# Stick-breaking attention: two value matmuls in place of three, with the columns added afterwards

## The chip, the cores and the metric

The kernel runs on one core of one Trainium2 chip. A core has a matmul engine (TensorE, PE in the profile, with its weight loads shown apart as PEld), three engines for elementwise work (VectorE: DVE, ScalarE: ACT, GpSimd: POOL), a queue for transfers (SP), and 16 DMA engines that carry them. The time is the device time of one run in microseconds (us). Matmul results land in PSUM, which is cut into banks of 512 fp32 columns; all other tiles lie in SBUF.

## The reference, cut to what matters

The program is one layer of a residual trunk with 2048 rows of 1024: a projection, four heads of differential attention, eight heads of stick-breaking attention, an output projection, and a gated feed-forward layer. The change touches stick-breaking attention alone:

```python
z = jnp.einsum('bqhd,bkhd->bhqk', qb, k).astype(jnp.float32) * scale      # 64 wide heads
log_1mb = jnp.where(mask, jax.nn.log_sigmoid(-z), 0.0)
rem = lax.cumsum(log_1mb, axis=3, reverse=True) - log_1mb
a = jnp.where(mask, jnp.exp(jax.nn.log_sigmoid(z) + rem), 0.0)            # probabilities
y = jnp.einsum('bhqk,bkhd->bqhd', a.astype(v.dtype), v)
y_sb = rms_norm(y, sb_out_norm_w)                                         # per head, over 64 columns
```

The mask is strictly causal, so row block i (128 rows, i from 0 to 15) needs i + 1 key blocks of 128.

## The kernel before, in words

Inputs are fp32, and matmuls run on pairs of fp16 numbers. A value a is held as a high part and a low part, and a product a times v is computed as high times high, high times low and low times high, all added in PSUM.

Work is done in eight groups. Groups 0 to 3 are the differential heads, and groups 4 to 7 hold two stick-breaking heads each (m = 0 and 1). While a group's attention runs, the projection of the next group (L320 on PE, with its results split on ACT and DVE, L327 and L330) runs between. In the last group the output projection takes that place (L761 on PE, L764 on DVE). The feed-forward layer follows from about 1500 us on.

A unit of stick-breaking attention is one row block i, one head m, and up to 1024 keys (b). `stage_a` makes its scores on PE in chunks of 512 keys (L448, with the mask added at L450). ACT takes two sigmoids of each chunk (L554 and L555), DVE a running product from the right (L557, the TENSOR_TENSOR_SCAN of the profile) and a product (L558). `split_t` makes the high part on ACT (L89) and the low part on POOL (L98) into a buffer s16 (three of them). A transposing DMA on SP's queue (L403) then brings both parts to the tile aT, in which keys lie on partitions: tiles j hold the high parts, and nb + j the low parts.

`stage_b` runs five units later. Its `pv` (L458) multiplies the 128x128 tiles of aT, as stationary operands, with the values, which lie side by side as 64 high and 64 low columns for each head. For each key block it has three matmuls of 64 columns, each with a weight load of its own, into the same 64 columns of the PSUM tile yp. One yp tile of 512 columns holds four row blocks with two heads each (two row blocks in group 7, where k is 2), and there are two such tiles in turn.

When the last row block of a yp tile is done, `finish` norms it: ACT squares it into an SBUF tile y (L418), DVE sums the squares (L419), ACT and POOL make the inverse root (L148, L151), DVE multiplies yp by it into y (L429), PE transposes y back into yp (L431), and ACT and DVE split the result (L435, L436), which goes out by DMA (L439).

The order of the instructions on each engine is fixed when the program is built. A scheduler places them by a modelled timeline, and every engine then works through its list in that order. A small planner (`note`, `pick`) adds up estimated nanoseconds for each engine and by them decides which of two engines takes some of the splits.

Of the kernel before, what the change touches and what calls it, by code (L numbers as in the profile page):

```python
# [59 lines left out]
def block(tc, a, out):  # L60
# [3 lines left out]
    with top:  # L64
# [8 lines left out]
        def note(e, ns):  # L73
            load[e] += ns * KW[e]
# [176 lines left out]
        with ExitStack() as ph1:  # L251
# [152 lines left out]
                return aT  # L404

            @pri("fin")
            def finish(g, G, i, k, yp, ssum=None):
                nh, w = (1, 128) if g < 4 else (2, 64)
                nr = k * nh
                yv = yp[:, : k * P].rearrange("p (r e) -> p r e", e=w)  # L410
                y = sp.tile([P, 512], F32, tag="y", bufs=2, name=nm("y"))
                y_ = y[:, : k * P].rearrange("p (r e) -> p r e", e=w)
                ss = sm.tile([P, 8], F32, tag="yss", name=nm("yss"))
                if nh == 1:
                    for r in range(nr):
                        ACT.activation(y_[:, r, :], yv[:, r, :], AF.Square, accum_out=ss[:, r : r + 1])
                else:
                    ACT.activation(y_, yv, AF.Square)  # L418
                    DVE.tensor_reduce(ss[:, :nr], y_, op=ALU.add, axis=AX.X)  # L419
                rs = sm.tile([P, 8], F32, tag="yrs", name=nm("yrs"))  # L420
                if ssum is None:
                    rstd(rs[:, :nr], ss[:, :nr], 1.0 / w, G["epsy"][:])
                else:
                    er = sm.tile([P, 4], F32, tag="er", name=nm("er"))
                    ACT.activation(er[:, :k], ssum[:, :k, 0], AF.Square, scale=G["rty"][:])
                    DVE.scalar_tensor_tensor(rs[:, :nr], ss[:, :nr], 1.0 / w, er[:, :k], op0=ALU.mult, op1=ALU.add)
                    POOL.tensor_scalar(rs[:, :nr], rs[:, :nr], 1e-37, 0.0, op0=ALU.max, op1=ALU.add)
                    POOL.tensor_tensor(rs[:, :nr], rs[:, :nr], mhalf[:, :nr], ALU.pow)
                DVE.tensor_tensor(y_, yv, rs[:, :nr].unsqueeze(2).to_broadcast([P, nr, w]), ALU.mult)  # L429
# [6 lines left out]
                DVE.scalar_tensor_tensor(mo[:, :k, 1, :], tr, gn, mo[:, :k, 0, :], op0=ALU.mult, op1=ALU.subtract)  # L436
# [15 lines left out]
            @pri("pv")  # L452
            def pv(G, yp, y0, aT, b, n, o, wd, start, stop):
                nb = n // P
                for j in range(nb):
                    v = G["v"][2 * b + j // 4][:, j % 4, :]
                    for q, (a_, v_) in enumerate(((j, o), (j, o + wd), (nb + j, o))):
                        PE.matmul(yp[:, y0 : y0 + wd], lhsT=aT[:, a_, :], rhs=v[:, v_ : v_ + wd], start=start and j == 0 and q == 0, stop=stop and j == nb - 1 and q == 2, skip_group_check=True)  # L458

            def diff_attn(g, G):  # L460
                @pri("at")
# [74 lines left out]
            def sb_attn(g, G):  # L536
                last = {}

                @pri("at")
                def stage_a(i, m, b):  # L540
                    L = (i + 1) * 128
                    n = min(1024, L - 1024 * b)
                    be, om = z4(), z4()
                    if b == i // 8:
                        DVE.memset(om[:, n : n + 1], 8192.0)
                    else:
                        DVE.tensor_copy(om[:, n : n + 1], last[m][:, 0:1])
                    last[m] = om
                    for c in range((n - 1) // 512, -1, -1):
                        lo, hi = 512 * c, min(512 * c + 512, n)  # L550
                        w = hi - lo
                        sc = ps.tile([P, 512], F32, tag="sc", bufs=4, name=nm("sc"))
                        score_chunk(G, sc, i, 2 * b + c, m, w // P, b == i // 8 and hi == n)
                        ACT.activation(om[:, lo:hi], sc[:, :w], AF.Sigmoid, scale=G["nkz"][:])  # L554
                        ACT.activation(sc[:, :w], sc[:, :w], AF.Sigmoid, scale=G["kz"][:])  # L555
                        ov = om[:, lo:hi][:, ::-1]
                        DVE.tensor_tensor_scan(ov, ov, sc[:, :w], om[:, hi : hi + 1], op0=ALU.mult, op1=ALU.bypass)  # L557
                        DVE.tensor_tensor(be[:, lo:hi], sc[:, :w], om[:, lo + 1 : hi + 1], ALU.mult)  # L558
# [4 lines left out]
                ypd = {}  # L563

                def stage_b(i, m, b, n, aT):
                    r, k = fq(g, i)
                    if i // k not in ypd:
                        ypd[i // k] = ps.tile([P, 512], F32, tag="yp", name=nm("yp"))
                    yp = ypd[i // k]
                    pv(G, yp, P * r + 64 * m, aT, b, n, 128 * m, 64, r == 0 and m == 0 and b == i // 8, r == k - 1 and m == 1 and b == 0)  # L570
                    if m == 1 and b == 0 and r == k - 1:
                        finish(g, G, i, k, yp)
                        G["fin"] = i + 1

                pend = []
# [12 lines left out]
                for u in pend:  # L588
                    stage_b(*u)
# [638 lines left out]
```

## Time and profile before

| what | value |
|---|---|
| time, median of 3 runs | 2782.47 us (2777.36 to 2783.66) |
| span of the profiled execution (the only time that its page gives) | 2785.0 us |
| PE busy | 2489.9 us (89%), 17084 matmuls |
| DVE busy | 2000.8 us (72%) |
| ACT busy | 1361.8 us (49%) |
| POOL busy | 1445.2 us (52%) |
| L458, matmuls of both kinds of attention | 4896 matmuls, 281.2 us |
| mean granted TensorE clock | 0.966 |

Busy time counts every moment in which an engine has an instruction under way. Matmuls are pipelined, so a single one shows some 200 ns while a row of them runs at a much closer pace. The span is an average over stages: from 0 to about 610 us the projection and the differential heads, to about 1200 us the stick-breaking heads with the projection, to about 1500 us the last group with the output projection, and then the feed-forward layer.

### The profile page before, as it was taken

What the parts mean: (1) busy time and instruction counts of PE and PEld (TensorE: products, weight loads), DVE (VectorE), ACT (ScalarE), POOL (GpSimd) and SP (SyncE); (2) the same over time, 40 slices, a digit from 0 to 9 for tenths busy, and PEclk for the clock granted to TensorE, in tenths of its full rate; (3) what the DMA queues carried; (4) which work ended last, traced back from release to release, by engine and by line L of the source; (5) the groups of instructions that cost most, each with busy time, mean ns of one, the idle gap of its engine ahead of it and who ended that gap; (6) DMA issues with size and microseconds to landing.
All of it is one profiled execution on the core that took longest, in us unless ns stands there. A gap on an engine that the chain in (4) does not pass through costs nothing. (4 is left out here: it accounts for less than half of the span.)

```text
span 2785.0 us, 45469 instructions
## 1 busy us (share of the span) xinstructions
PE 2489.9 (89%) x17084; PEld 1409.0 (51%) x17084; DVE 2000.8 (72%) x3782; ACT 1361.8 (49%) x2543; POOL 1445.2 (52%) x1008
## 2 busy tenths in 40 slices
PE   6998989888878786888889798989999999999998
PEld 4665556555545453557775343444444444444443
DVE  6888879687989989876756877777786644434445
ACT  4665656466878788765644534443442212111121
POOL 2567767665544555546665656565654332322323
PEclk9999999999999897999999999999999999999999
DMA  6788787789999998997796565655658844635534
GB/s 225 199 167 184 147 188 163 164 174 205 198 205 198 192 182 160 190 198 205 197 309 253 184 235 189 221 187 191 240 170 299 327 155 178 227 125 190 211 129 166
DMA packets 649133, 551.91 MB, mean 198 GB/s; under 512 B 506624, under 2 KB 574208, under 8 KB 638672
## 3 DMA queue, kind: packets, MB, share of 16 engines
q1 hardware_dynamic: 647088, 546.92, 71.2%
q8 instruction: 134, 2.20, 0.3%
q0 software_dynamic: 512, 1.36, 0.2%
q10 hardware_dynamic: 1312, 0.72, 0.1%
q14 instruction: 87, 0.71, 0.1%
HBM read 265.27 MB, written 151.52 MB: 150 GB/s over the span
## 5 line engine op out<-in xcount | busy, mean ns | idle before, releaser
L98 POOL TENSOR_TENSOR s<-z,s 128x1024 f16<-128x1024 f32 (+7 forms) x288 | 474.1, 1654 | 334.8 <-ACT s L89 299.3
L320 PE MATMUL pj<-w,xt 128*128 128x384 f16 x3072 | 572.3, 334 | 32.6 <-DVE st L330 11.6
L320 PEld LDWEIGHTS <-xt 128*128 128x128 f16 x3072 | 299.9, 100 | 241.8 <-issue 36.3
L448 PE MATMUL sc<-kT,qT 128*128 128x512 f16 (+3 forms) x1280 | 346.9, 362 | 74.6 <-DVE z L558 34.4
L1034 PE MATMUL pd<-wd,act 128*128 128x512 f16 x1848 | 406.2, 379 | 3.3 <-DVE hs L1040 2.4
L557 DVE TENSOR_TENSOR_SCAN z<-z,sc 128x512 f32<-128x512 f32 (+3 forms) x320 | 355.5, 1112 | 68.6 <-ACT sc L555 65.1
L458 PE MATMUL yp<-v,aT 128*128 128x64 f16 (+1 forms) x4896 | 281.2, 207 | 80.0 <-DMA aT<-s 79.2
L458 PEld LDWEIGHTS <-aT 128*128 128x128 f16 x4896 | 245.2, 102 | 169.4 <-DMA aT<-s 105.1
L936 PEld LDWEIGHTS <-wg 128*128 128x128 f16 x1848 | 183.9, 100 | 264.3 <-issue 58.8
L98 POOL TENSOR_TENSOR hs<-hs,cu 128x512 f32<-128x512 f32 x132 | 170.5, 1297 | 238.2 <-DVE cu L1040 82.6
L936 PEld LDWEIGHTS <-wu 128*128 128x128 f16 x1848 | 181.0, 98 | 222.1 <-issue 9.0
L1034 PEld LDWEIGHTS <-act 128*128 128x128 f16 x1848 | 180.6, 98 | 222.6 <-issue 4.7
L98 POOL TENSOR_TENSOR act<-cg,act 128x512 f16<-128x512 f32 x117 | 160.8, 1385 | 247.7 <-ACT act L992 141.5
L98 POOL TENSOR_TENSOR fst<-fst 128x512 f32<-128x512 f32 x97 | 179.6, 1852 | 167.6 <-DVE wd L215 78.6
L1040 DVE SCALAR_TENSOR_TENSOR hs<-pd,c,hs 128x512 f32<-128x512 f32 x192 | 142.1, 748 | 160.8 <-PE pd L1034 159.1
L89 ACT CAST s<-z 128x384 f16<-128x384 f32 (+7 forms) x216 | 170.1, 788 | 151.5 <-DMA aT<-s 56.4
L554 ACT ACTIVATE z<-sc,c 128x512 f32<-128x512 f32 (+3 forms) x320 | 202.6, 633 | 10.6 <-PE sc L448 6.5
L558 DVE TENSOR_TENSOR z<-sc,z 128x512 f32<-128x512 f32 (+3 forms) x320 | 193.3, 606 | 8.1
L992 ACT CAST act<-cg 128x512 f16<-128x512 f32 x132 | 80.6, 617 | 234.2 <-DVE cg L998 190.9
L555 ACT ACTIVATE sc<-sc,c 128x512 f32<-128x512 f32 (+3 forms) x320 | 194.8, 609 | 0.0
L761 PE MATMUL po<-wo,mt 128*128 128x256 f16 x1536 | 181.3, 276 | 11.0 <-DVE xf L764 6.3
L936 PE MATMUL pm<-X,wg 128*128 128x512 f16 x792 | 179.1, 379 | 1.2 <-ACT bx L1109 1.2
(233 smaller groups left out, 4028.4 us busy)
## 6 DMA issues: line engine op xcount, KB each, us to landing
xt<-xs SPq DMA_DIRECT2D x112, 512.0 KB, 4.4
hs<-hd SPq DMA_DIRECT2D x96, 512.0 KB, 4.3
hd<-hs SPq DMA_DIRECT2D x80, 512.0 KB, 3.2
split<-wg SPq DMA_DIRECT2D x11, 1792.0 KB, 10.5
split<-wu SPq DMA_DIRECT2D x11, 1792.0 KB, 10.3
split<-wd SPq DMA_DIRECT2D x11, 1792.0 KB, 10.4
wg<-split SPq DMA_DIRECT2D x11, 1792.0 KB, 7.3
wd<-split SPq DMA_DIRECT2D x11, 1792.0 KB, 8.4
```

What stands on the lines that cost most here:

```text
L89: ACT.copy(dst, src)
L98: (DVE if e == "D" else POOL).tensor_tensor(dst, a_, b_, op)
L320: PE.matmul(pj[:, :384], lhsT=xv[:, xi, kt, :], rhs=G["w"][:, wi, kt, :], start=n == 0, stop=n == 23)
L448: PE.matmul(sc[:, : 128 * w].rearrange("p (t n) -> p t n", n=P), lhsT=G["q"][i // 4][:, 2 - 2 * o + m, i % 4, :], rhs=G["k"][q][:, m, 0:w, ...
L458: PE.matmul(yp[:, y0 : y0 + wd], lhsT=aT[:, a_, :], rhs=v[:, v_ : v_ + wd], start=start and j == 0 and q == 0, stop=stop and j == nb - 1 a ...
L554: ACT.activation(om[:, lo:hi], sc[:, :w], AF.Sigmoid, scale=G["nkz"][:])
L555: ACT.activation(sc[:, :w], sc[:, :w], AF.Sigmoid, scale=G["kz"][:])
L557: DVE.tensor_tensor_scan(ov, ov, sc[:, :w], om[:, hi : hi + 1], op0=ALU.mult, op1=ALU.bypass)
L558: DVE.tensor_tensor(be[:, lo:hi], sc[:, :w], om[:, lo + 1 : hi + 1], ALU.mult)
L761: PE.matmul(po[:, sl], lhsT=mt[:, kt, P * xi : P * xi + P], rhs=wos[2 * h + n][wi][:, kt, :], start=q == 0, stop=q == 23)
L936: PE.matmul(ps_[:].rearrange("p (t n) -> p t n", n=P), lhsT=wv[:, wo, wi, 128 * kt : 128 * kt + 128], rhs=X[xo][:, :, xi, kt, :], start=st ...
L1034: PE.matmul(po[:], lhsT=act[:, ao, xi, 128 * j : 128 * j + 128], rhs=W["d"][:, wo, wi, :], start=start and u == 0 and q == 0, stop=u == nu ...
```

## The change

The three matmuls of 64 columns for a key block become two (`pv_joined`). The first multiplies the high part of the probabilities with the high and the low values side by side, 128 columns, so that high times high and high times low land in two neighbouring parts of 64 columns. The second adds low times high to the first of these parts. A head of a row block takes 128 columns of yp for that, so a yp tile now holds two row blocks, and there is one for every second row block.

When a tile is complete, `add_parts` copies the second parts (4 x 64 columns) on ACT into an SBUF tile, and DVE adds the first parts from PSUM and that copy into another SBUF tile y. `finish` then works from y, uses the tile of copies for the squares, and still transposes into yp. The SBUF pool y has three buffers where it had two. `add_parts` notes 400 ns for ACT and 350 ns for DVE in the planner.

```diff
-            def finish(g, G, i, k, yp, ssum=None):
+            def finish(g, G, i, k, yp, ssum=None, parts=None):
...
+                if parts is None:
+                    y = sp.tile([P, 512], F32, tag="y", bufs=3, name=nm("y"))
+                    src, sq = yp, y
+                else:
+                    y, sq = parts
+                    src = y
+                yv, y_, sq_ = (z[:, : k * P].rearrange("p (r e) -> p r e", e=w) for z in (src, y, sq))
...
+            @pri("pv")
+            def pv_joined(G, yp, y0, aT, b, n, m, start, stop):
+                nb = n // P
+                for j in range(nb):
+                    v = G["v"][2 * b + j // 4][:, j % 4, 128 * m : 128 * m + 128]
+                    PE.matmul(yp[:, y0 : y0 + 128], lhsT=aT[:, j, :], rhs=v, start=start and j == 0, stop=False, skip_group_check=True)
+                    PE.matmul(yp[:, y0 : y0 + 64], lhsT=aT[:, nb + j, :], rhs=v[:, :64], start=False, stop=stop and j == nb - 1, skip_group_check=True)
+
+            @pri("fin")
+            def add_parts(yp, y, tmp, h):
+                yv = yp[:].rearrange("p (r s e) -> p r s e", r=4, s=2)
+                y_, t_ = (z[:, 256 * h : 256 * h + 256].rearrange("p (r e) -> p r e", r=4) for z in (y, tmp))
+                ACT.copy(t_, yv[:, :, 1, :])
+                DVE.tensor_tensor(y_, yv[:, :, 0, :], t_, ALU.add)
+                note("A", 400)
+                note("D", 350)
...
-                    if i // k not in ypd:
-                        ypd[i // k] = ps.tile([P, 512], F32, tag="yp", name=nm("yp"))
-                    yp = ypd[i // k]
-                    pv(G, yp, P * r + 64 * m, aT, b, n, 128 * m, 64, r == 0 and m == 0 and b == i // 8, r == k - 1 and m == 1 and b == 0)
+                    if i // k not in ysum:
+                        ysum[i // k] = [sp.tile([P, 512], F32, tag="y", bufs=3, name=nm("y")) for _ in range(2)]
+                    if i // 2 not in ypd:
+                        ypd[i // 2] = ps.tile([P, 512], F32, tag="yp", name=nm("yp"))
+                    yp = ypd[i // 2]
+                    pv_joined(G, yp, 256 * (i % 2) + 128 * m, aT, b, n, m, i % 2 == 0 and m == 0 and b == i // 8, i % 2 == 1 and m == 1 and b == 0)
+                    if m == 1 and b == 0 and i % 2 == 1:
+                        add_parts(yp, *ysum[i // k], r // 2)
                     if m == 1 and b == 0 and r == k - 1:
-                        finish(g, G, i, k, yp)
+                        finish(g, G, i, k, yp, None, ysum[i // k])
```

Over the whole program 3264 matmuls of 64 columns become 1088 of 128 and 1088 of 64, with as many weight loads. ACT gains 32 copies and DVE 32 additions. One subtraction of 512 columns in the last group's output projection (L98) moves from DVE to POOL by the planner.

In ACT's list, at a place in the middle of the stick-breaking groups, the order before is this (sc and z are a chunk's scores and sigmoids, s the high parts that go to the transposing DMA):

```order
L554 ACTIVATE z_11644<-sc_11653,c_8304 128x512
L555 ACTIVATE sc_11653<-sc_11653,c_8303 128x512
L89 CAST s_11632<-z_11615 128x1024
L554 ACTIVATE z_11727<-sc_11729,c_8304 128x512
L555 ACTIVATE sc_11729<-sc_11729,c_8303 128x512
L89 CAST s_11660<-z_11643 128x1024
L554 ACTIVATE z_11767<-sc_11769,c_8304 128x512
L555 ACTIVATE sc_11769<-sc_11769,c_8303 128x512
L89 CAST s_11737<-z_11726 128x512
```

and with the change (where L554 and L555 have become L575 and L576, and L476 is the new copy):

```order
L575 ACTIVATE z_11316<-sc_11325,c_8304 128x512
L576 ACTIVATE sc_11325<-sc_11325,c_8303 128x512
L89 CAST s_11306<-z_11289 128x1024
L575 ACTIVATE z_11391<-sc_11393,c_8304 128x512
L576 ACTIVATE sc_11393<-sc_11393,c_8303 128x512
L89 CAST s_11332<-z_11315 128x1024
L476 COPY y_11109<-yp_11110 128x256
L575 ACTIVATE z_11425<-sc_11427,c_8304 128x512
L576 ACTIVATE sc_11427<-sc_11427,c_8303 128x512
L89 CAST s_11401<-z_11390 128x512
```

The copy is put between a cast and the sigmoids of the next unit; the rest stands as before.

In DVE's list at the same place the order before is this (the running product L557 is listed as SCALAR_TENSOR_TENSOR):

```order
L557 SCALAR_TENSOR_TENSOR z_11644<-z_11644,sc_11653 128x512
L558 TENSOR_TENSOR z_11643<-sc_11653,z_11644 128x512
L557 SCALAR_TENSOR_TENSOR z_11727<-z_11727,sc_11729 128x512
L558 TENSOR_TENSOR z_11726<-sc_11729,z_11727 128x512
L545 MEMSET z_11767 128x1
L178 TENSOR_REDUCE m_13132<-wsc_13128 128x1
L557 SCALAR_TENSOR_TENSOR z_11767<-z_11767,sc_11769 128x512
```

and with the change (L578, L579 and L566 are the L557, L558 and L545 of before):

```order
L578 SCALAR_TENSOR_TENSOR z_11316<-z_11316,sc_11325 128x512
L579 TENSOR_TENSOR z_11315<-sc_11325,z_11316 128x512
L578 SCALAR_TENSOR_TENSOR z_11391<-z_11391,sc_11393 128x512
L579 TENSOR_TENSOR z_11390<-sc_11393,z_11391 128x512
L566 MEMSET z_11425 128x1
L477 TENSOR_TENSOR y_11108<-yp_11110,y_11109 128x256
L178 TENSOR_REDUCE m_12636<-wsc_12632 128x1
```

The addition L477 is put between the running products of two units; nothing else has moved there. Elsewhere the steps of `finish` stand a little later than before in the same lists: on POOL, the inverse root (L151) is mostly put one subtraction (L98) further down.

More of the change, by code (lines that the diff above doesn't have):

```diff
@@ L406, in finish @@
             @pri("fin")
-            def finish(g, G, i, k, yp, ssum=None):
+            def finish(g, G, i, k, yp, ssum=None, parts=None):
                 nh, w = (1, 128) if g < 4 else (2, 64)
                 nr = k * nh
-                yv = yp[:, : k * P].rearrange("p (r e) -> p r e", e=w)
-                y = sp.tile([P, 512], F32, tag="y", bufs=2, name=nm("y"))
-                y_ = y[:, : k * P].rearrange("p (r e) -> p r e", e=w)
+                if parts is None:
[5 more added lines that the diff above has]
+                yv, y_, sq_ = (z[:, : k * P].rearrange("p (r e) -> p r e", e=w) for z in (src, y, sq))
                 ss = sm.tile([P, 8], F32, tag="yss", name=nm("yss"))
@@ L415, in finish @@
                     for r in range(nr):
-                        ACT.activation(y_[:, r, :], yv[:, r, :], AF.Square, accum_out=ss[:, r : r + 1])
+                        ACT.activation(sq_[:, r, :], yv[:, r, :], AF.Square, accum_out=ss[:, r : r + 1])
                 else:
-                    ACT.activation(y_, yv, AF.Square)
-                    DVE.tensor_reduce(ss[:, :nr], y_, op=ALU.add, axis=AX.X)
+                    ACT.activation(sq_, yv, AF.Square)
+                    DVE.tensor_reduce(ss[:, :nr], sq_, op=ALU.add, axis=AX.X)
                 rs = sm.tile([P, 8], F32, tag="yrs", name=nm("yrs"))
@@ L561, in stage_a @@
                     return n, split_t(be[:, :n], n, "A", "P")
-                ypd = {}
+                ypd, ysum = {}, {}
                 def stage_b(i, m, b, n, aT):
                     r, k = fq(g, i)
-                    if i // k not in ypd:
-                        ypd[i // k] = ps.tile([P, 512], F32, tag="yp", name=nm("yp"))
-                    yp = ypd[i // k]
-                    pv(G, yp, P * r + 64 * m, aT, b, n, 128 * m, 64, r == 0 and m == 0 and b == i // 8, r == k - 1 and m == 1 and b == 0)
+                    if i // k not in ysum:
[6 more added lines that the diff above has]
+                        add_parts(yp, *ysum[i // k], r // 2)
                     if m == 1 and b == 0 and r == k - 1:
-                        finish(g, G, i, k, yp)
+                        finish(g, G, i, k, yp, None, ysum[i // k])
                         G["fin"] = i + 1
```

## The prediction, made before the changed kernel was run

> **What bounds the kernel now.** Only the stick-breaking stage (about 615 to 1420 us) is touched, so I read it by stretches first: the busy time of the engines from 615 to 1200 us, where the projection still runs beside the attention, and from there to the end of the last group. The scans' own row (L557, first and last start 618.2 and 1401.1 us) gives the stage's bounds.
>
> ```profile
> core 0: us, PE busy (x) PEld busy (x) DVE busy (x) ACT busy (x) POOL busy (x), PEclk, DMA share, GB/s
> 615.00:1200.00 585.00, 464.16 (x4777) 292.29 (x4775) 520.26 (x932) 458.09 (x881) 304.51 (x196) 0.93 0.96 192
> 1200.00:1420.00 220.00, 194.53 (x2059) 160.58 (x2057) 151.91 (x247) 131.42 (x227) 130.20 (x87) 0.97 0.81 203
> 1420.00:1500.00 80.00, 72.21 (x545) 54.64 (x543) 44.37 (x83) 33.80 (x39) 37.80 (x27) 0.98 0.88 330
> ...
> L557 DVE TENSOR_TENSOR_SCAN z<-z,sc x320: 453/1270/1282, 618.2 to 1401.1; 128x512 f32<-128x512 f32 x88, 128x128 f32<-128x128 f32 x24, 128x256 f32<-128x256 f32 x24, 128x384 f32<-128x384 f32 x24
> ...
> 650.00:700.00 50.00, 42.12 (x405) 26.69 (x403) 38.78 (x72) 38.98 (x77) 18.64 (x13) 0.97 1.10 225
> 750.00:800.00 50.00, 41.44 (x446) 25.79 (x443) 49.47 (x87) 40.35 (x71) 28.86 (x15) 1.00 1.10 216
> ```
>
> Up to 1200 us DVE is the fullest engine: 520.26 of 585 us, 0.89. PE has 0.79 and ACT 0.78. After 1200 us it is the other way round: PE 0.88, DVE 0.69. The DMA engines are nearly full too (0.96), though 0.96 is not their ceiling, since two slices show 1.10.
>
> Then I read who waits for whom from 615 to 1200 us.
>
> ```profile
> DVE z L557 <- ACT sc L555: 33.5, 41, 3.2
> ...
> PE yp L458 <- DMA aT<-s: 41.4, 39, 3.3
> PE sc L448 <- DVE z L558: 32.6, 31, 2.0
> PE sc L448 <- DVE z L545: 16.7, 19, 1.9
> ...
> ACT s L89 <- DMA aT<-s: 33.6, 28, 4.2
> ...
> SPq L403 <- POOL s L98: 160.4, 89, 6.8
> ```
>
> PE makes its next scores only when DVE has given back a buffer (32.6 + 16.7 us). DVE waits for ACT's sigmoids 33.5 us. The value matmuls wait 41.4 us for transposes, and behind nothing that they make does DVE or ACT stand. SP's transposes in turn wait 160.4 us for POOL, so the transfers are short of work at times and don't set the pace alone. I take DVE as the pace up to 1200 us, and PE after it.
>
> **The change, part by part. The matmuls.** A key block had three matmuls of 64 columns; it gets one of 128 and one of 64, 192 columns in either case. What is saved is one matmul's fixed part. Rows of the timeline show the pace of an unbroken run (start, length, count):
>
> ```profile
> 565.11 1.06 PE L458 MATMUL yp<-v,aT 128*128 128x128 f16 x16
> ...
> 1020.27 0.70 PE L458 MATMUL yp<-v,aT 128*128 128x64 f16 x18 [0.56 <-DMA aT<-s]
> ...
> 1043.32 1.46 PE L458 MATMUL yp<-v,aT 128*128 128x64 f16 x24 [3.20 <-DMA aT<-s]
> ```
>
> Taking off the last one's own length (about 0.19 us for 64 columns and 0.22 us for 128, by the rows below), 18 matmuls of 64 columns take (0.70 - 0.19) / 17 = 30 ns each, and 16 of 128 columns (1.06 - 0.22) / 15 = 56 ns. So a key block goes from 3 x 30 = 90 ns to 56 + 30 = 86 ns: 4 ns. The third row is a stretch after an idle PE at a lower granted clock, (1.46 - 0.19) / 23 = 55 ns each, where I expect no gain either, since nearly all of that is columns. Both paces have the weight loads in them.
>
> ```profile
> L458 PE MATMUL yp<-v,aT 128*128 128x64 f16 x2616 | 123.6, 201 | 39.3 <-DMA aT<-s 39.0 <-DVE mo L436 0.2
> L458 PE MATMUL yp<-v,aT 128*128 128x128 f16 x132 | 9.2, 219 | 2.4 <-DMA aT<-s 2.4
> ...
> L458 PE MATMUL yp<-v,aT 128*128 128x64 f16 x648 | 27.7, 194 | 10.0 <-DMA aT<-s 9.9
> ```
>
> The first two rows are of 615 to 1200 us, the third of 1200 to 1420 us. 2616 / 3 = 872 key blocks lie in the first stretch: 872 x 4 ns = 3.5 us, hidden, since PE then waits longer for DVE. 648 / 3 = 216 lie in the second: 0.9 us, which I count. The other end for this price is busy time: 123.6 / 2616 = 47 ns for 64 columns and 9.2 / 132 = 70 ns for 128, thus 3 x 47 - (70 + 47) = 24 ns for a block, 26 us over all 1088. It counts the trailing length of every short run as work, so I take the 4 ns and keep the 24 for a rival.
>
> The Trainium skill, "TensorE: Matmul & The Clock Gate", section "Back-to-back issue gap", gives about 81 ns for a matmul of 128 columns in a sustained stream of weight loads and matmuls. The trace has 56 ns for just such a stream. By the Trainium skill's figure a block would go from 90 ns up to 81 + 30 = 111 ns, and the joining would be a loss on PE; by the row it is even.
>
> **The new elementwise work.** 32 times ACT copies 256 columns from PSUM, and DVE adds 256 columns of PSUM and 256 of SBUF into SBUF. The nearest rows of 615 to 1200 us:
>
> ```profile
> L558 DVE TENSOR_TENSOR z<-sc,z 128x256 f32<-128x256 f32 x28 | 11.7, 418 | 0.7
> L429 DVE TENSOR_TENSOR y<-yp,yrs 128x512 f32<-128x512 f32 x13 | 8.8, 678 | 0.4 <-POOL yrs L428 0.3
> L429 DVE TENSOR_TENSOR y<-yp,yrs 128x256 f32<-128x256 f32 x3 | 1.2, 415 | 1.5 <-POOL yrs L151 1.5
> ...
> L327 ACT ACTIVATE st<-pj 128x256 f16<-128x256 f32 x55 | 21.7, 394 | 17.4 <-DVE v L330 16.8 <-DVE m L195 0.6
> L418 ACT ACTIVATE y<-yp 128x512 f32<-128x512 f32 x12 | 7.4, 617 | 0.0
> L418 ACT ACTIVATE y<-yp 128x256 f32<-128x256 f32 x3 | 1.2, 403 | 0.0
> ```
>
> L558 has the very operands of the addition: 418 ns. L418 reads 256 columns of the same PSUM tile in 403 ns. So DVE gains 32 x 0.418 = 13.4 us and ACT 32 x 0.40 = 12.9 us. Twelve tiles of `finish` with four row blocks (24 additions) and three with two lie before 1200 us by the counts of L418, thus 27 additions, 27 x 0.418 = 11.3 us of DVE; the other five (2.1 us) fall where DVE is 0.69 busy and PE sets the pace, and I cost them at nothing. If DVE set the pace there too, they would cost 2.1 us.
>
> How much of the 11.3 us reaches the end? DVE's spare time before 1200 us is 0.11, and an addition that falls into a wait is free: 0.89 x 11.3 = 10.1 us. In the two slices with a DMA share of 1.10 (100 of 585 us) the transfers may set the pace: 485 / 585 x 10.1 = 8.4 us. ACT's copies lie beside DVE's work; ACT has 127 us to spare here. Where DVE waits for ACT they count, and DVE's additions don't, at nearly the same price, so I count only one of the two. The ends: nothing, if the transfers cover everything, and 27 x (0.418 + 0.40) = 22 us, if each pair counts in full.
>
> **The steps of `finish` that read another place.** L418 and L429 read SBUF in place of PSUM. A cast of 512 columns from SBUF and a DVE subtraction of 1024 columns from SBUF stand at
>
> ```profile
> L89 ACT CAST s<-z 128x512 f16<-128x512 f32 x14 | 8.8, 631 | 1.6 <-DMA aT<-s 1.4 <-DVE z L545 0.3
> ...
> L98 DVE TENSOR_TENSOR x<-z,x 128x1024 f16<-128x1024 f32 x4 | 5.3, 1329 | 0.0
> ```
>
> so 631 against 617 ns and about 665 against 678 ns: over 20 tiles less than 0.3 us either way, taken as nothing. The one subtraction of 512 columns that goes from DVE to POOL frees about 0.7 us of DVE after 1200 us, where DVE has slack: nothing. The chain from the last matmul of a tile to its transpose grows by a copy and an addition, 0.8 us. Ahead of it PE still has rows of other units and of the output projection, and the output projection has some 72 us of PE work left after 1420 us (the third row above), so this is nothing as well; without that cover it would be 0.8 us once, at the end.
>
> **PSUM tiles.** With half as many row blocks to a tile, a tile's turn comes twice as often. A tile is free once `finish` has done L436, and now one other tile of two row blocks lies between, not four row blocks. The list before shows a wait of 0.2 us for L436 (the row of 2616 matmuls above). At a group's start the row blocks are short, and I allow 0 to 2 us for each of three starts, taken as 0.
>
> **The sum.** +8.4 - 0.9 = +7.5 us. Against the profiled execution's span, 2785.0 us, this is 2792.5; against the median of the runs, which lies 2.5 us under that span, 2790.0 us.
>
> **The rivals.**
>
> *The transfers hide it.* The DMA share is 0.96 over the stretch, ACT waits 33.6 us for a buffer that a transpose has to release, and the value matmuls 41.4 us. If transposes set the pace in more of the stage than the two full slices, say in two thirds of it, then 10.1 / 3 = 3.4 us remain, less 0.9: about 2785 us, no change that can be told. Against it stand the 160.4 us in which the transposes wait for POOL, and behind POOL for ACT and DVE.
>
> *PE is what sets the pace, and fewer matmuls shorten it.* This is the other side: faster. In busy time a block saves 24 ns. If PE set the pace in half of the stretch before 1200 us and throughout after it, that is 0.5 x 872 x 24 ns + 216 x 24 ns = 10.5 + 5.2 = 15.7 us, against half of DVE's 10.1 us: -10.7, or 2772 us. It decides once PE sets the pace in about a third of that stretch. For it speaks PE's 0.88 after 1200 us, and against it that matmuls of 64 columns run at 30 ns wherever a run is long enough to show a pace, and that PE itself waits for DVE for over 49 us.
>
> *The copies hold up ACT.* The copy stands in ACT's list ahead of the next unit's sigmoids, and must wait for the last value matmul of its tile, which waits for a transpose (41.4 us over 39 waits, 1.06 us each). If each of the 27 copies waited that long, with DVE behind it on the sigmoids, 27 x 1.06 = 29 us come on top of 7.5: 2819 us; with a third of them, 2800. Before, the squares L418 waited for the same matmuls in the same way, and their rows show 0.0 us of idle time, which is why I give it little.
>
> *The matmul of 128 columns is dear.* By its 70 ns of busy time against the 30 ns pace, a block would take 70 + 30 = 100 ns in place of 90: 216 x 10 ns = 2.2 us after 1200 us, where PE sets the pace, in place of the 0.9 gained, thus 2793 us. With the Trainium skill's 81 ns it would be 216 x 21 ns = 4.5 us, and 2795 us.
>
> **How the numbers follow.** DVE's additions count: 0.43, 2790 us, of its own 2786 to 2796. The transfers hide it: 0.32, 2785 (2781 to 2788). PE sets the pace: 0.15, 2772 (2765 to 2777). Copies hold up ACT: 0.06, 2800 and over. Dear matmuls: 0.04, 2793. What a measurement of this kernel can tell from no change is 0.2%, 5.6 us, so faster means under 2777 and slower over 2788. Slower: 0.34 of the first case's 0.43, 0.02 of the second, and the last two, 0.46. Faster: the third nearly whole, 0.14, and 0.02 of the second, 0.16. The same: 0.38. The range from 2777 to 2800 leaves out the third case and the far part of the fourth, 2 in 10 together.
>
> **What would show it.** If I am right, L458's successors together take nearly what the 123.6 + 27.7 us of before were in runs of the same length (30 and 56 ns apart), the addition takes some 420 ns and the copy some 400, DVE's busy time up to the last scan grows by about 13 us, the last scan (1401 us before) comes some 8 us later, and PE's waits for DVE at the scores grow. If the last scan stands where it stood and the DMA share is higher, the transfers hid the work. If the stretch after 1200 us is shorter by over 5 us, PE's count of matmuls mattered. Waits of ACT at the copy for PE would show the fourth case. A change in the feed-forward part (after 1500 us) would be none of these, and would make the prediction wrong in its ground.

## The result, and the profile after

The changed kernel takes 2787.02 us (median of 16 runs, 2782.19 to 2791.59) against 2780.84 us for the kernel before in the same comparison (16 runs, 2776.09 to 2788.75). The ratio is 1.0022, with a 95% interval of 1.0013 to 1.0030: slower by some 6 us, where 7.5 us was forecast.

A caution comes first. The profiled execution of the changed kernel took 2783.75 us, 3.3 us under its median, and its span is 2782.0 us. The profiled execution of before has a span of 2785.0 us, and with as much beside it (1.75 us) a time 4.3 us over the median of its first runs. So the two profiles, laid side by side, show 3 us of gain. They can be read for what each instruction costs and for whom it waits, but not for where 6 us went.

The busy time by stretches, cut at the first and the last scan of each kernel, before:

```profile
core 0: us, PE busy (x) PEld busy (x) DVE busy (x) ACT busy (x) POOL busy (x), PEclk, DMA share, GB/s
0.00:618.00 618.00, 543.54 (x4122) 348.37 (x4123) 508.08 (x1467) 358.85 (x902) 393.93 (x302) 0.96 0.78 179
618.00:1402.00 784.00, 638.45 (x6578) 434.62 (x6576) 660.65 (x1163) 577.98 (x1089) 417.51 (x273) 0.94 0.92 194
1402.00:2785.00 1383.00, 1307.88 (x6388) 626.04 (x6386) 832.10 (x1154) 424.93 (x553) 633.77 (x435) 0.98 0.58 209
```

and after:

```profile
0.00:612.00 612.00, 540.53 (x4116) 345.61 (x4117) 508.40 (x1467) 358.43 (x902) 394.11 (x302) 0.97 0.78 181
612.00:1397.00 785.00, 645.50 (x5517) 430.19 (x5515) 681.95 (x1194) 586.08 (x1120) 420.00 (x273) 0.92 0.91 193
1397.00:2782.00 1385.00, 1311.00 (x6369) 626.46 (x6367) 831.82 (x1154) 425.32 (x554) 633.62 (x436) 0.98 0.58 209
```

The first stretch, which the change hardly touches, differs by 6 us. The stick-breaking stage takes 784 and 785 us, although DVE is busy in it for 681.95 us in place of 660.65: 21.3 us more busy time, and 1 us more time. DVE's idle time took the rest (123 us before, 103 us after). Not all of the 21.3 us is new work: three groups of DVE's instructions that the change leaves alone (two of L215, one of L223) take 7.8 us longer in the profile after.

The matmuls came out as forecast. A run of them after, from the timeline (the tail of each, 0.19 or 0.22 us, overlaps the next):

```profile
1018.03 0.19 PE L470 MATMUL yp<-v,aT 128*128 128x64 f16 x1
1018.06 0.22 PE L469 MATMUL yp<-v,aT 128*128 128x128 f16 x1
...
1018.38 0.19 PE L470 MATMUL yp<-v,aT 128*128 128x64 f16 x1
```

Four key blocks lie between the first of these rows and the last, 0.35 us, thus 88 ns a block at this resolution: 86 were forecast, and 90 stood before. The elementwise work is in the rows of the tile y, after and before (minimum, median and maximum in ns):

```profile
L476 ACT COPY y<-yp x32: 350/394/501, 642.8 to 1411.6; 128x256 f32<-128x256 f32 x32
L477 DVE TENSOR_TENSOR y<-yp,y x32: 397/402/425, 643.3 to 1412.0; 128x256 f32<-128x256 f32 x32
...
L433 DVE TENSOR_TENSOR y<-y,yrs x20: 403/677/2402, 668.8 to 1418.8; 128x512 f32<-128x512 f32 x12, 128x256 f32<-128x256 f32 x8
```

```profile
L429 DVE TENSOR_TENSOR y<-yp,yrs x21: 406/669/691, 649.7 to 1421.6; 128x512 f32<-128x512 f32 x13, 128x256 f32<-128x256 f32 x8
```

The copy (394 ns) and the addition (402 ns) cost what the nearest rows said (403 and 418). The multiply of `finish` (L429 before, L433 after) has nearly the same median (677 and 669 ns), but its longest is 2402 ns where it was 691. That was not foreseen, and the last section takes it up.

Who waits, in the changed kernel, for the instructions that write or read y there (us and times):

```profile
  ACT y L422: 9.2, 5
...
  ACT yrs L148: 1.3, 4
```

and in the kernel before:

```profile
  ACT yrs L148: 8.1, 9
```

The first row is new: ACT's square waits 9.2 us in 5 waits, and the same view names DVE's addition L477 as what it waits for. In the kernel before, the square waited for PE alone, 0.4 us. But another wait of ACT for DVE in `finish` shrank at the same time: the scaling (L148), which waits for DVE's sums, went from 8.1 to 1.3 us. Both together are 8.1 us before and 10.5 us after. DVE's waits for ACT's sigmoids, 33.5 us before 1200 us, are 33.1 us after.

### The profile page after: what moved, and what is told of

The parts are those of the page before. It is cut to its first block, busy times and chain, and to the rows that moved or that the text cites. A ratio compares the mean times of both kernels' runs of the same rounds, so it can differ in the third digit from the quotient of the medians.

```text
span 2782.0 us, 43359 instructions
## 1 busy us (share of the span) xinstructions
PE 2497.0 (90%) x15996; PEld 1402.3 (50%) x15996; DVE 2022.2 (73%) x3813; ACT 1369.8 (49%) x2575; POOL 1447.7 (52%) x1009
## 5 line engine op out<-in xcount | busy, mean ns | idle before, releaser
L98 POOL TENSOR_TENSOR s<-z,s 128x1024 f16<-128x1024 f32 (+7 forms) x288 | 473.0, 1650 | 329.4 <-ACT s L89 299.5
L578 DVE TENSOR_TENSOR_SCAN z<-z,sc 128x512 f32<-128x512 f32 (+3 forms) x320 | 355.9, 1113 | 57.6 <-ACT sc L576 55.1
L98 POOL TENSOR_TENSOR hs<-hs,cu 128x512 f32<-128x512 f32 x132 | 170.4, 1296 | 237.0 <-DVE hs L1065 79.7
L98 POOL TENSOR_TENSOR act<-cg,act 128x512 f16<-128x512 f32 x117 | 161.3, 1390 | 246.1 <-ACT act L1017 139.5
L98 POOL TENSOR_TENSOR fst<-fst 128x512 f32<-128x512 f32 x97 | 182.2, 1878 | 171.8 <-DVE wd L215 77.6
L575 ACT ACTIVATE z<-sc,c 128x512 f32<-128x512 f32 (+3 forms) x320 | 204.2, 638 | 7.3 <-PE sc L452 5.8
L579 DVE TENSOR_TENSOR z<-sc,z 128x512 f32<-128x512 f32 (+3 forms) x320 | 193.0, 606 | 7.3
L576 ACT ACTIVATE sc<-sc,c 128x512 f32<-128x512 f32 (+3 forms) x320 | 196.4, 614 | 0.0
L786 PE MATMUL po<-wo,mt 128*128 128x256 f16 x1536 | 181.7, 276 | 11.1 <-DVE xf L789 5.2
L469 PE MATMUL yp<-v,aT 128*128 128x128 f16 x1088 | 135.4, 232 | 57.1 <-DMA aT<-s 51.6
L452 PEld LDWEIGHTS <-qT 128*128 128x128 f16 x1280 | 107.6, 100 | 144.4 <-DVE z L579 47.6
```

Source lines behind the costliest of these rows:

```text
L98: (DVE if e == "D" else POOL).tensor_tensor(dst, a_, b_, op)
L452: PE.matmul(sc[:, : 128 * w].rearrange("p (t n) -> p t n", n=P), lhsT=G["q"][i // 4][:, 2 - 2 * o + m, i % 4, :], rhs=G["k"][q][:, m, 0:w, ...
L786: PE.matmul(po[:, sl], lhsT=mt[:, kt, P * xi : P * xi + P], rhs=wos[2 * h + n][wi][:, kt, :], start=q == 0, stop=q == 23)
```

## The experiments

All ratios are against the kernel before on the same chip in the same comparison; chips differ by some 4 us (the kernel before takes 2780.71 us on one and 2784.38 us on another). At this kernel's length 0.001 is 2.8 us.

| kernel | ratio | 95% interval |
|---|---|---|
| the change | 1.0022 | 1.0013 to 1.0030 |
| three matmuls again, parts and additions kept | 1.0040 | 1.0025 to 1.0056 |
| no additions | 0.9984 | 0.9974 to 0.9994 |
| additions five times | 1.0066 | 1.0052 to 1.0079 |
| copies five times | 1.0058 | 1.0044 to 1.0071 |
| step by way of DVE, without the work | 1.0034 | 1.0021 to 1.0047 |
| DVE's work, without the step | 0.9990 | 0.9980 to 1.0000 |
| without the 1088 matmuls of 64 columns | 0.9973 | 0.9959 to 0.9986 |
| square put further down | 1.0032 | 1.0021 to 1.0043 |
| squares on DVE | 1.0003 | 0.9993 to 1.0013 |
| squares and scaling on DVE | 1.0047 | 1.0028 to 1.0065 |
| before, in another order | 0.9974 | 0.9962 to 0.9986 |
| before, scaling on DVE | 1.0016 | 1.0006 to 1.0026 |

The theory of the prediction was that DVE's additions cost, since DVE sets the pace. The first rivals were the matmuls, ACT's copies, and transfers that hide everything.

**The matmuls apart.** The edit:

```diff
-                    PE.matmul(yp[:, y0 : y0 + 128], lhsT=aT[:, j, :], rhs=v, start=start and j == 0, stop=False, skip_group_check=True)
+                    PE.matmul(yp[:, y0 : y0 + 64], lhsT=aT[:, j, :], rhs=v[:, :64], start=start and j == 0, stop=False, skip_group_check=True)
+                    PE.matmul(yp[:, y0 + 64 : y0 + 128], lhsT=aT[:, j, :], rhs=v[:, 64:], start=False, stop=False, skip_group_check=True)
```

> The changed kernel, but with three matmuls of 64 columns for a key block again (high times low lands in the second part by a matmul of its own); the two parts, the copies and the additions stay. If DVE's additions are what the change costs, the joining is worth 4 ns for each of 1088 key blocks at most, mostly hidden: 0 to 3 us over the changed kernel (2787 to 2790 us). If the matmuls of 128 columns are what made it slower (a dear matmul between two loads), this is back at the kernel before, some 2781 us. If the joining had saved the busy time of a matmul (24 ns a block, 26 us in all) and the additions had cost it again, this is 10 us or more over the changed kernel.

Measured: 1.0040, 0.0018 over the change, or 5 us, between the 0 to 3 us of the first case and the 10 us of the third. There is no sign that the matmul of 128 columns is dear, since this kernel would then have come out faster than the change. The 5 us is more than the 4.4 us of PE that joining saves in all. By the control further down, a difference of this size can come from the order alone, so the worth of the joining is known only as between nothing and somewhat over 10 us.

**Without the additions.**

```diff
-                ACT.copy(t_, yv[:, :, 1, :])
-                DVE.tensor_tensor(y_, yv[:, :, 0, :], t_, ALU.add)
+                ACT.copy(y_, yv[:, :, 0, :])
```

> The changed kernel without DVE's additions: ACT copies the first part (256 columns, as many as before) into y, and the second part, high times low, is left out of the result. If DVE sets the pace, 27 additions of 0.40 us that lie before 1200 us come off, times 0.75 to 0.9: 8 to 10 us under the changed kernel, 2777 to 2780 us. If it is ACT's copies and their waits, it stays at the changed kernel's 2787 us. If transfers hide the additions and the 6 us come from elsewhere, also 2787 us.

Measured: 0.9984, which is 0.0038 (10.6 us) under the change, just over what the theory expected: 12.9 us of DVE's work gone and 10.6 us of time. Taken alone, it would have settled the matter.

**The additions five times.**

```diff
-                DVE.tensor_tensor(y_, yv[:, :, 0, :], t_, ALU.add)
+                for _ in range(5):
+                    DVE.tensor_tensor(y_, yv[:, :, 0, :], t_, ALU.add)
```

> The changed kernel with each addition made five times into the same tile: 128 more additions of 0.40 us, 51 us more of DVE, of which 43 us before 1200 us. If DVE sets the pace there: 0.75 to 0.9 of 43 us, and 0 to 5 us from the rest, thus 32 to 44 us over the changed kernel, 2819 to 2831 us. If the transfers set the pace and DVE's spare time takes the additions: under 15 us, below 2802 us. If only the waits around the copies matter: under 10 us.

Measured: 1.0066, 0.0044 over the change (12.2 us, by the two intervals some 7.5 to 17) where 32 to 44 us were expected. The stage of this kernel:

```profile
617.00:1419.00 802.00, 656.66 (x5503) 436.43 (x5502) 715.89 (x1318) 586.78 (x1120) 421.08 (x273) 0.90 0.89 189
```

DVE is busy 34 us more than in the changed kernel's stage (715.89 against 681.95), and the stage is 17 us longer in these two executions. By the medians, 128 additions of 0.413 us (the median row of the line), 52.9 us, cost 12.2 us: 0.23 us of time for each us of listed duration. A listed duration is more than an addition takes from DVE, though, since the next instruction starts before it is over. A place in this kernel's timeline:

```profile
1038.03 0.42 DVE L478 TENSOR_TENSOR y<-yp,y 128x256 f32<-128x256 f32 x1
1038.36 0.47 DVE L579 TENSOR_TENSOR_SCAN z<-z,sc 128x128 f32<-128x128 f32 x1
```

The addition lasts 0.42 us, and the next instruction starts 0.33 us after it did. Over the additions with such a successor the median step is 0.32 us, so the 128 take some 41 us of DVE by this estimate, and the price is 0.30. By either count DVE does not set the pace one for one. At 0.23 the single additions of the change, 12.9 us of listed duration, would cost 3 us and not 10.6.

**The copies five times.**

```diff
-                ACT.copy(t_, yv[:, :, 1, :])
+                for _ in range(5):
+                    ACT.copy(t_, yv[:, :, 1, :])
```

> The changed kernel with each copy on ACT made five times into the same tile: 128 more copies of 0.39 us, 50 us more of ACT, of which 42 us before 1200 us. If DVE sets the pace, ACT's 127 us to spare take most of it; only where DVE waits for ACT (33 us of waits, 0.06 of the stretch) does it count: 0 to 12 us over the changed kernel, 2787 to 2799 us. If ACT's chain of sigmoids and casts sets the pace as much as DVE, 25 to 40 us, 2812 to 2827 us.

Measured: 1.0058, 0.0036 over the change (10 us): 50 us of ACT by listed duration cost 0.20 us for each us, within what was expected, and hardly less than DVE's price. Here too the next instruction starts early: the median step from a copy to its successor is 0.26 us where a copy lasts 0.39, which makes some 34 us and a price of 0.30. By these two prices neither engine sets the pace alone.

So the first addition seemed to cost 10.6 us and the next four 12.2 us together. This led to a second theory: what costs is the new wait in ACT's list (the square L422 behind the addition L477, 9.2 us), not the work. Two kernels part the wait from the work.

**The step by way of DVE without its work, and the work without the step.** Both start from the kernel without additions. The first adds the step alone, the second the work alone:

```diff
+                DVE.tensor_copy(y_[:, 0, 0:1], yv[:, 0, 0, 0:1])
```

```diff
+                DVE.tensor_tensor(yv[:, :, 1, :], yv[:, :, 0, :], y_, ALU.add)
```

> As the kernel without additions (ACT copies the first part into y, high times low is left out of the result), but DVE writes one column of y after the copy, so that ACT's square still has to wait for DVE as it does in the changed kernel: the step by way of DVE stays, and its work (0.40 us each) is nearly gone. If the additions cost by DVE's time, this is at the kernel without additions and some 1 to 3 us more, 2777 to 2780 us. If they cost by the new wait (ACT's square for DVE's addition: 9.2 us in 5 waits of the changed kernel's profile), it is near the changed kernel, 2784 to 2788 us.

> As the kernel without additions (high times low is left out), but DVE makes an addition of the same 256 columns whose result (in the second part of the PSUM tile) no one reads: DVE's work stays, and ACT's square waits for no addition. If the additions cost by DVE's time, this is near the changed kernel, 2784 to 2789 us. If they cost by the new wait, it is near the kernel without additions, 2776 to 2780 us.

Measured: 1.0034 for the step without the work, and 0.9990 for the work without the step. The work costs 0.0006 (1.7 us, not told from nothing) against the kernel without additions, and the step 0.0050 (14 us). Taken alone, that speaks for the second theory and against the first. The control below takes most of its weight away.

**Without the low part's matmuls.** The line of the 1088 matmuls of 64 columns is taken out, and the mark for a finished tile (stop) moves to the line above it:

```diff
-                    PE.matmul(yp[:, y0 : y0 + 128], lhsT=aT[:, j, :], rhs=v, start=start and j == 0, stop=False, skip_group_check=True)
-                    PE.matmul(yp[:, y0 : y0 + 64], lhsT=aT[:, nb + j, :], rhs=v[:, :64], start=False, stop=stop and j == nb - 1, skip_group_check=True)
+                    PE.matmul(yp[:, y0 : y0 + 128], lhsT=aT[:, j, :], rhs=v, start=start and j == 0, stop=stop and j == nb - 1, skip_group_check=True)
```

> The changed kernel without its 1088 matmuls of 64 columns (low times high is left out of the result): 33 us less of PE by the pace of 30 ns, 26 us of it before 1200 us and 6.5 us after. If DVE sets the pace before 1200 us and PE after it, 3 to 8 us under the changed kernel, 2779 to 2784 us. If PE's work counts throughout, as the 5 us between the unjoined kernel and the changed one suggest for only 4.4 us of PE, 20 to 33 us under it, 2754 to 2767 us.

Measured: 0.9973, 0.0049 under the change: 13.6 us for 33 us of PE, 0.41 us for each us, between the two expectations. PE counts in part too, by this number rather more than DVE and ACT. It is a net price: the granted clock in the stage was 0.89 here and 0.92 with the change, and PE's busy time in the whole program fell by 18.7 us (2497.0 to 2478.3), not by 33.

**The square put further down.**

```diff
-                    ACT.activation(sq_, yv, AF.Square)
+                    with tc.issue_after(sig[0].ins):
+                        ACT.activation(sq_, yv, AF.Square)
```

Here sig is the last sigmoid written so far, and `finish` is written one unit later.

> The changed kernel with the whole computation, in which finish is written after the next unit's value matmuls and ACT's square is put behind the sigmoids of the unit made last, one or two units further down in some of the lists. If the new wait of the square for the addition is what costs, some of its 9 us go: 2781 to 2785 us, and that wait shrinks in the profile. If DVE's time costs, 2785 to 2789 us, no change against the changed kernel.

Measured: 1.0032, no better than the change. The rows of the tile y show who waits there now:

```profile
  ACT yrs L148: 11.0, 8
...
  ACT y L425: 0.7, 1
```

The square (now L425) waits 0.7 us in place of 9.2, but ACT's scaling, the next step of `finish` on ACT, waits 11.0 us for DVE's sums in place of 1.3. The wait has moved by one step and is no smaller. The stage takes 784 us where the changed kernel's took 785:

```profile
614.00:1398.00 784.00, 643.10 (x5503) 429.17 (x5502) 680.18 (x1193) 585.30 (x1119) 412.21 (x273) 0.93 0.90 193
```

The part after the last scan has 1394 us where the changed kernel had 1385. The last tiles' `finish` is written later here too, which may delay the output projection that needs them; that wasn't tried apart. So this run says little of the second theory.

**No waits of ACT for DVE in `finish`, and a control.** Three more kernels were meant to take such waits away, and the fourth is a control with nothing added or taken away. The squares on DVE, in the changed kernel:

```diff
-                    ACT.activation(sq_, yv, AF.Square)
+                    DVE.tensor_tensor(sq_, yv, yv, ALU.mult)
```

The scaling on DVE, once with the squares there, and once alone in the kernel before:

```diff
-                    rstd(rs[:, :nr], ss[:, :nr], 1.0 / w, G["epsy"][:])
+                    DVE.tensor_scalar(rs[:, :nr], ss[:, :nr], 1.0 / w, G["epsy"][:], op0=ALU.mult, op1=ALU.add)
+                    POOL.tensor_tensor(rs[:, :nr], rs[:, :nr], mhalf[:, :nr], ALU.pow)
```

The control, the kernel before with another priority of `finish`:

```diff
-PRI = {"sc": 0, "spl": 0, "pv": 0, "fin": 0, "pm": -200, "po": 0, "pb": 0, "lw": 0, "fr": 0, "at": 200, "ox": 0, "wm": 0}
+PRI = {"sc": 0, "spl": 0, "pv": 0, "fin": -20, "pm": -200, "po": 0, "pb": 0, "lw": 0, "fr": 0, "at": 200, "ox": 0, "wm": 0}
```

> The changed kernel with the whole computation, in which DVE makes the squares of finish (y times y, 20 tiles, some 11 us of DVE more) in place of ACT, so that no instruction of ACT waits for an addition. If the changed kernel lost by that wait, this is 0.996 to 0.9995 of the kernel before (1 to 11 us under it), about where the kernel with DVE's work and without the step by way of DVE stood (0.999). If it lost by DVE's time, 11 us more of DVE make it slower still: 1.004 to 1.006. If any other order of the same instructions moves the time as much, it may lie anywhere from 0.998 to 1.004.

> As the one with DVE's squares, and the scaling ahead of the inverse root (ACT's L148, which waits for DVE's sums) is made on DVE as well, 20 small instructions of about 0.2 us. Then no step of finish has ACT waiting for DVE. If such waits are what costs: 0 to 6 us less than with DVE's squares alone, 0.994 to 0.9985 of the kernel before. If DVE's time costs: 3 to 4 us more than with DVE's squares alone.

> The kernel before (three matmuls, no additions) with the scaling ahead of the inverse root made on DVE, so that ACT does not wait for DVE's sums there (8.1 us in 9 waits before). If ACT's waits for DVE within finish cost, it is 0.997 to 0.9995 of the kernel before. If DVE's time costs (20 instructions of about 0.2 us, 4 us), 1.000 to 1.0015.

> A control: the kernel before with the same instructions and the same waits between them, in which finish has another priority (-20 in place of 0), so that the scheduler makes another order of the lists, differing from the old one in about as many rows as the changed kernel does. If the waits and the work that were added are what cost, this is 0.999 to 1.001 of the kernel before. If a new order alone moves the time by as much as the change did, it lies outside of 0.9985 to 1.0015.

Measured: squares on DVE 1.0003, with the scaling as well 1.0047, the scaling alone in the kernel before 1.0016, and the control 0.9974. The squares on DVE lie a little above the 0.996 to 0.9995 of the second theory, and within what a new order was allowed. Their profile shows the wait moved once more: ACT's scaling waits 10.4 us for DVE's sums, in 10 waits, where the changed kernel had 1.3. With the scaling on DVE as well, the time rose by 0.0044, over both expectations; alone in the kernel before it rose by 0.0016, at the upper end of what DVE's 4 us would cost. ACT's waits for DVE's sums are gone in both (8.1 us in 9 waits before). But POOL's inverse root, which waited 6.4 us for the scaling before, waits longer now that it hangs on DVE, in the second of these kernels:

```profile
POOL yrs L423 <- DVE yrs L422: 20.1, 11, 5.2
```

With the squares there too it is 17.1 us. So these two kernels put a longer wait on POOL in place of the one on ACT, and do not settle the second theory either.

The control decides how much of all this can be read. The same instructions with the same dependences, in another order, are 0.0026 (7 us) faster than before, as much as the change is slower. Its stage, to be laid beside the 784 us of before:

```profile
618.00:1390.00 772.00, 636.18 (x6510) 428.75 (x6508) 664.34 (x1148) 574.29 (x1085) 410.04 (x271) 0.93 0.91 195
```

12 us came off in the stage itself in this execution, with DVE's busy time no smaller (664.34 against 660.65), and nothing before it (618 us in both) or after it (1384 us against 1383).

**What follows.** Each of these kernels was scheduled anew, and so each has an order of its own. In the one case measured a new order was worth 7 us. If each of two kernels can have that much from its order, a difference of up to 14 us between them cannot be put down to the edit alone. That covers the single additions (10.6 us) and the step (14 us), and also the five additions (12.2 us), the five copies (10 us) and the missing matmuls (13.6 us), so all these prices are rough. A bound stands even so: the five additions would have cost 33 us at the price of the prediction, 0.63 us for each us of listed duration, and even if the order had hidden all of 14 us, they would cost 26 us, a price of 0.5.

The second theory isn't shown. The pair of the step and the work speaks for it, and none of the four kernels that were to test it took the wait away: it went to another step or to POOL. ACT's waits for DVE at the square and the scaling together, 10.5 us with the change, are 11.1 us with five additions and 4.4 us with five copies (waits of single executions), and both kernels are slower than the change by more than 9 us. So that sum does not tell the time either.

The control is also the one kernel with the whole computation that beats both: 0.9974 of the kernel before.

## Why the prediction was right or wrong

Right in direction and in size: 7.5 us forecast, 6.2 us measured by the medians, both just over the 5.6 us that was called the least difference to be told. Its cause is not shown by that, and one step fell.

- *The matmuls, 4 ns a block.* The pace was right: some 88 ns in the trace against 86 forecast, and no sign of the dear matmul, or of busy time being saved. That PE's savings before 1200 us are hidden was probably too strong. By the missing matmuls each us of PE is worth about 0.4 us, with what two orders can do on the 13.6.
- *DVE's additions, 402 ns where 418 was taken.* Right as a duration. It is too much as the time that an addition takes from DVE, by the steps of 0.32 us between an addition and its successor.
- *"How much of the 11.3 us reaches the end?"* This is the step that failed. It took DVE's busy share (0.89) as the share of new work that reaches the end, less the two slices with full transfers and the five additions after 1200 us. That made 8.4 us of 13.4, or 0.63 us for each us. Five additions in place of one measured 0.23, whose upper end is near 0.32 by the intervals, and 0.5 with the whole 14 us of two orders. A busy share is not a price. PE, ACT, DVE and the transfers all have over 0.7 of the stage here, and each waits for the others by turns. That new work in any of them goes in part into its own waits fits DVE's idle time, 20 us shorter after, but no run shows it apart from the order.
- *ACT's copies counted at nothing beside DVE's additions.* Probably mis-sized: by the five copies 0.20 us for each us, 2.5 us for 12.6 us.
- *The steps that read another place, "taken as nothing".* Mis-sized. The multiply of `finish` takes 4.8 us more in the stage, as worked out in the last section. No run took that away alone.
- *PSUM tiles, "taken as 0".* PE's wait for a tile that `finish` gives back (L436 before, L440 after) grew from 0.2 us to 4.9 us, in two waits. In other kernels with the same tiles it is anything from nothing (without additions) to 5.5 us (the step without the work). No run went back to tiles of four row blocks, so the share of this wait in the 6 us is not known.
- *The copies hold up ACT.* The wait of that rival was small: the rows for the tiles show ACT waiting 4.3 us for the value matmuls at the copies. The wait that did come was another, the square's for the addition. The prediction counted no wait there, and the scaling's wait shrank by 6.8 us beside it.
- *The scheduler's new order.* Left out of the prediction altogether: no rival had it, and it is as large as the forecast.
- *The signs that it named.* Copy, addition and the pace of the matmuls came as named. Three others did not. The last scan was to come 8 us later. It came at 1396.1 us in place of 1401.1, and counted from the first scan it is 783.6 us after and 782.9 before. DVE's busy time was to grow by 13 us and grew by 21.3. PE's waits for DVE at the scores were to grow, and from 615 to 1200 us they are 57.6 us before and 58.0 after. Since the two profiles lie 3 us apart the wrong way round, this speaks against the mechanism only weakly.

With the measured prices, 0.23 for DVE (12.9 us and the 4.8), 0.20 for ACT and 0.41 for PE (-4.4 us), an estimate of the change is 4.1 + 2.5 - 1.8 = +4.8 us, before the order. The order can move that by 7 us either way, so that the forecast came so near is partly luck. Where the 6 us lie stays open: the two profiles differ by as much in a stretch that the change hardly touches, and no run held the order fixed while the additions went.

## What to carry to other kernels

In this kernel, where three engines and the transfers are each busy for seven tenths of a stage or more, the price of new work was well under its duration on each of them. Such a price is better measured by putting the same work in several times over, since a single removal lies within what a new order does. Where a scheduler decides the order, one control with the same work in another order belongs to the first experiments, not to the last. And a kernel that is to take a wait away tests nothing until its profile shows that the wait has not gone to the next step.

## What the runs showed of the hardware

Moving an operand of a DVE instruction from PSUM to SBUF made it wait for POOL. Before, the multiply of `finish` read yp from PSUM; now it reads y from SBUF. Its rows in the stage, before and after:

```profile
L429 DVE TENSOR_TENSOR y<-yp,yrs 128x512 f32<-128x512 f32 x13 | 8.8, 678 | 0.4 <-POOL yrs L428 0.3
L429 DVE TENSOR_TENSOR y<-yp,yrs 128x256 f32<-128x256 f32 x7 | 2.9, 417 | 2.8 <-POOL yrs L151 2.8
```

```profile
L433 DVE TENSOR_TENSOR y<-y,yrs 128x512 f32<-128x512 f32 x12 | 10.8, 904 | 0.2 <-POOL yrs L151 0.2
L433 DVE TENSOR_TENSOR y<-y,yrs 128x256 f32<-128x256 f32 x7 | 5.0, 712 | 3.2 <-POOL yrs L151 3.2
```

In the mean this is 904 against 678 ns and 712 against 417: 12 x 226 + 7 x 295 ns = 4.8 us of DVE. Six of the 20 are longer, and each of the six begins while POOL is in a subtraction (L98). One such place of the timeline after (start and length in us):

```profile
704.33 2.12 POOL L98 TENSOR_TENSOR s<-z,s 128x1024 f16<-128x1024 f32 x1 [0.62 <-ACT s L89]
...
705.59 1.41 DVE L433 TENSOR_TENSOR y<-y,yrs 128x512 f32<-128x512 f32 x1
```

and one of the timeline before, with yp in PSUM:

```profile
1309.02 2.13 POOL L98 TENSOR_TENSOR s<-z,s 128x1024 f16<-128x1024 f32 x1 [2.00 <-ACT s L89]
...
1309.17 0.41 DVE L429 TENSOR_TENSOR y<-yp,yrs 128x256 f32<-128x256 f32 x1
```

After, POOL's instruction ends at 706.45 us, and the multiply 0.55 us later, at 707.00. A second pair ends at 997.70 and 998.25 us, again 0.55 us apart. So in both places the multiply of 512 columns does its own half microsecond of work once POOL is done, however early it began. Before, the multiply begins 0.15 us into a subtraction of 2.13 us and takes its usual 0.41 us. The additions, which read one operand from PSUM and one from SBUF, stay between 397 and 425 ns throughout. The Trainium skill has this rule, in "SBUF — State Buffer", section "Who interferes with whom": a DVE instruction with two SBUF inputs and a GpSimd instruction that reads SBUF exclude each other, and whichever began second waits for the whole of the first. The trace agrees, with the two places after. In `finish`, y and the row scales yrs are both in SBUF, and the prediction missed it by comparing durations alone.

The other thing not expected is the size of the order's effect: 7 us of 2784, with no instruction added, taken away or made to wait for another result.
